# RMS norms of a two-layer S5/FoX decoder trunk: root on VectorE, first half early, S5 input matrices a tile ahead

## The chip, the core and the metric

The kernel runs on one core of a Trainium2 chip. A core has five engines with an instruction queue each: TensorE (PE; its weight loads are shown as PEld), VectorE (DVE), ScalarE (ACT), GpSimd (POOL) and SyncE (SP, which here only issues DMAs). The metric is the device time of one execution in microseconds; the median of several executions counts.

## The reference

One sequence of 512 tokens of 1024 channels passes through two layers. Layer 0 is an S5 state-space mixer, layer 1 a FoX (forgetting) attention; behind each stands a gated ConvFFN. Each of the four sub-layers is normed and modulated, and its output is gated and added to the residual:

```python
def rmsnorm(x, g):
    y = x32 * lax.rsqrt(jnp.mean(x32 * x32, axis=-1, keepdims=True) + EPS)
    return y * g
def adaln_params(c, w, b):
    mod = jax.nn.silu(c) @ w + b            # 1024 x 3072, per sub-layer
    shift, scale, gate = jnp.split(mod, 3, axis=-1)
def modulate(x, g, shift, scale):
    return rmsnorm(x, g) * (1.0 + scale) + shift
# S5: u = h @ w_in; a diagonal complex recurrence per group of 16 channels;
#     y = gelu(y + d_skip * u); y = y * sigmoid(y @ w_glu); y @ w_out
# FoX: softmax attention with a decay bias; ConvFFN: silu(conv3(a)) * b, then w_down
```

A last RMS norm without modulation (gain `final_g`) gives the output. All of it is float32.

## The kernel before

**Layout.** The residual `h` lies with channels on partitions: 8 tiles of 128 channels by 512 tokens. A norm's sum over channels is therefore a sum over partitions and tiles, made on TensorE; its result, one number a token, has to come back as a row that is equal on all partitions. Tokens are also taken in two halves of 256.

**Products.** Nearly all products are made in three passes of split operands (`w_hi·a_hi`, `w_hi·a_lo`, `w_lo·a_hi`; the matmuls of line 228). Weights come through `raw`, ScalarE makes the high part (line 211), VectorE the low part (line 212). The products of the S5 mixer's input (line 854) and the small S5 products are plain float32.

**Norms.** `add_residual` (line 290) adds a tile to `h`, `square` squares it on ScalarE and sums squares on VectorE into `ssq` (lines 282 and 284). `rms_stats` (line 299) makes the column sums on TensorE (line 307, matmuls with one output column), ScalarE takes them out of PSUM with the mean and epsilon (`v`, line 312), and GpSimd works out the inverse root from an integer first guess and two correction steps (lines 316 to 327) and writes 128x128 diagonals `dg` (line 330). Only for the second half of the last norm is VectorE used in its place. `rms_rows` (line 333) multiplies a matrix of ones with the diagonals, which gives the row (line 336). `norm_mod`'s `apply` (line 344) then does eight tiles: VectorE scales by gain and row (line 353), ScalarE adds the shift and makes the high part (line 356), VectorE the low part (line 357).

**Order at a norm.** The last product ahead of a norm works its two last weight tiles half by half (`tail`, lines 259 to 271). Between the halves stands the first half's `rms_stats`; after the second half, first `apply` of half 0 (its row matmul in it), then `rms_stats` of half 1. Half 1's `apply` is kept back (`pending`) and put in by `finish_norm` after the first 12 k-steps of the next product. A scheduler makes the final order in each engine's queue from this program order and from `issue_after`.

**The start.** `x` comes by four DMAs. The squares of the eight tiles are summed four and four on GpSimd and VectorE (line 820) and two sums go to `rms_stats` (line 307). VectorE meanwhile works through the S5 parameters (`s5_params`, lines 459 to 610), hundreds of small operations on 128x32. `ada_pe` (line 144) takes the conditioning's shift and scale, 16 weight tiles of 512 KB through three rings of buffers, on TensorE (line 155), two thirds side by side in four column groups; the 512-wide result is transposed to columns (`ada_columns`, lines 120 to 137; transposes line 126, VectorE's sum with the bias line 129). Then VectorE scales 16 tiles of 128x256 (line 840) and ScalarE adds the shift (line 843).

**The S5 loop.** For m = 0..7 (groups of 128 channels) the program order is: `s5_inputs(m)` (VectorE makes `x` from tables, lines 664 and 680; TensorE line 692; ScalarE takes `w` and `kt` out, lines 699 and 703; `kt` goes to memory `z` and comes back as Toeplitz tiles `tw`, which ScalarE masks into `t`, line 716), `outputs(m-1)` (TensorE lines 773 with `t`, 781 with the states; ScalarE's gelu, line 787, result to memory `yd`), `inputs(m+2)` (the product, line 854), some steps of conditioning (line 155: the third for the gate alone, in two column groups, then two thirds of the next sub-layer), `s5_scan(m)` (TensorE line 731) and the state output tables. `parts` reads `yd` back turned (`yt`) and splits it (lines 869 and 870), and `glu_head` works the first four glu tiles as parts arrive (line 228). The last tile's outputs, parts and glu steps come at the end with nothing behind them to fill TensorE.

**The end.** `norm_out` (line 363): ScalarE multiplies by the gain (line 373), the row is copied out (line 376), GpSimd (and for the second half VectorE too) multiplies with the row (line 380), and eight DMAs write the output channel-major (line 382).

## Time and profile before

| | |
|---|---|
| median of 3 runs | 1293.18 us (1292.35 to 1293.24) |
| profiled execution | 1296.91 us, of which the span of the trace is 1295.1 us |
| mean granted TensorE clock | 0.986 |
| VectorE, ScalarE, GpSimd instructions | 1343, 932, 215 |
| DMA | 183.11 MB, mean 141 GB/s |

The span is the time from the first to the last instruction of the profiled execution; what lies around it is 1.8 us. "Busy" is the sum of an engine's instruction times. In the rows that follow, `<-` names the instruction that ended a wait, `x` the number of instructions, and the last numbers of a windows row are the granted clock, the busy share of the DMA engines, and GB/s. A plain float32 matmul leaves two records, a split one a record for each of its three passes.

### The profile page before, as it was taken

The numbers are of one execution on the slowest core, as the hardware profiler recorded it, in microseconds if no ns is written. First come the engines' busy times: TensorE is split into PE (matmuls) and PEld (weight loads), VectorE is DVE, ScalarE is ACT, GpSimd is POOL, SyncE is SP. The second block draws the span as 40 slices with busy tenths as digits, with TensorE's granted clock in tenths as the row PEclk, the third lists the DMA queues.
The fourth block names the chain that finished last, engine by engine and source line by source line (L and its number), as shares of the span: only waits on it lengthen the run. The fifth ranks groups of instructions, "written<-read, shape, count | busy, mean of one in ns | idle before, by whom it ended". The sixth has DMA issues, their size and how long they took to land.

```text
span 1295.1 us, 17586 instructions
## 1 busy us (share of the span) xinstructions
PE 1246.3 (96%) x6728; PEld 1006.1 (78%) x6728; DVE 773.0 (60%) x1343; ACT 507.8 (39%) x932; POOL 98.6 (8%) x215
## 2 busy tenths in 40 slices
PE   4999999999999999999999999999999999999995
PEld 1466687898777778778899787878888888888885
DVE  8989975468665546765556567655754433444333
ACT  2344644334333223333333566644533312333331
POOL 3000000010000000000020243320200000000003
PEclk9999997999999999999999999999999999999998
DMA  9887665317665656655504433323233234332221
GB/s 350 294 260 212 185 189 165 109 55 212 213 187 154 187 145 220 194 160 157 157 2 132 154 123 127 97 70 98 63 119 92 68 92 133 95 96 85 73 66 65
DMA packets 74083, 183.11 MB, mean 141 GB/s; under 512 B 23079, under 2 KB 27519, under 8 KB 72975
## 3 DMA queue, kind: packets, MB, share of 16 engines
q1 hardware_dynamic: 73999, 181.99, 45.5%
q8 instruction: 53, 0.87, 0.3%
q14 instruction: 31, 0.25, 0.1%
HBM read 175.04 MB, written 6.92 MB: 140 GB/s over the span
## 4 chain that ended last, share of the span: by engine, by line
PE 70%; ACT 5%; DVE 4%; DMA 3%; issue 2%; POOL 2%; POOLq 0%; ACTq 0%; DVEq 0%; SPq 0%
PE mmp L228 64%; PE mmp L991 2%; ACT s L1102 2%; PE aux L1133 2%; DVE w_lo L212 1%; DMA raw<-in_w_up 1%; ACT w_hi L211 1%; PE aux L1116 1%; POOL hg L380 1%; PE aux L185 0%; DMA raw<-in_fox_qk 0%; ACT v L211 0%; DVE s L1098 0%; DVE ot L1140 0%; DMA raw<-in_ada_w 0%
## 5 line engine op out<-in xcount | busy, mean ns | idle before, releaser
L228 PE MATMUL mmp<-a_hi,w_hi 128*128 128x512 f32 (+1 forms) x944 | 363.6, 386 | 2.8 <-ACT a_hi L869 2.5
L228 PE MATMUL mmp<-a_lo,w_hi 128*128 128x512 f32 (+1 forms) x944 | 360.3, 382 | 0.9 <-DVE a_lo L870 0.9
L228 PE MATMUL mmp<-a_hi,w_lo 128*128 128x512 f32 (+1 forms) x944 | 360.4, 382 | 0.0
L212 DVE TENSOR_TENSOR w_lo<-raw,w_hi 128x1024 fp32r<-128x1024 f32 (+3 forms) x201 | 223.8, 1115 | 219.5 <-ACT w_hi L211 216.4
L211 ACT ACTIVATE w_hi<-raw 128x1024 fp32r<-128x1024 f32 (+3 forms) x201 | 194.6, 971 | 406.7 <-PE mmp L228 272.8
L228 PEld LDWEIGHTS mmp<-a_hi,w_hi 128*128 128x128 f32 x944 | 179.3, 190 | 43.0 <-issue 5.9
L228 PEld LDWEIGHTS mmp<-a_hi,w_lo 128*128 128x128 f32 x944 | 179.6, 190 | 34.0
L228 PEld LDWEIGHTS mmp<-a_lo,w_hi 128*128 128x128 f32 x944 | 179.6, 190 | 33.8 <-DVE a_lo L870 1.7
L228 PE MATMUL mmp<-ghi,w_hi 128*128 128x512 f32 (+1 forms) x396 | 147.5, 372 | 0.0
L228 PE MATMUL mmp<-glo,w_hi 128*128 128x512 f32 (+1 forms) x396 | 147.2, 372 | 0.0
L228 PE MATMUL mmp<-ghi,w_lo 128*128 128x512 f32 (+1 forms) x396 | 147.0, 371 | 0.0
L290 DVE SCALAR_TENSOR_TENSOR h<-mmp,par,h 128x512 f32<-128x512 f32 (+1 forms) x56 | 37.4, 673 | 110.2 <-PE mmp L228 110.1
L228 PEld LDWEIGHTS mmp<-ghi,w_hi 128*128 128x128 f32 x396 | 74.9, 189 | 15.8 <-issue 1.7
L228 PEld LDWEIGHTS mmp<-glo,w_hi 128*128 128x128 f32 x396 | 74.9, 189 | 14.1
L228 PEld LDWEIGHTS mmp<-ghi,w_lo 128*128 128x128 f32 x396 | 74.9, 189 | 14.0
L316 POOL TENSOR_SCALAR rs_i<-rs_v 128x2 int32<-128x2 int32 (+1 forms) x8 | 1.9, 235 | 1018.4 <-ACT rs_v L312 1018.4
L179 DVE SCALAR_TENSOR_TENSOR ada_acc<-raw,sc,ada_acc 128x1024 f32<-128x1024 f32 x49 | 62.7, 1280 | 19.3 <-DMA raw<-in_ada_w 19.0
L404 DVE SCALAR_TENSOR_TENSOR conv<-mmp,conv_wb,conv 128x511 f32<-128x511 f32 (+1 forms) x88 | 65.3, 745 | 4.3 <-ACT conv L402 3.1
L411 DVE TENSOR_TENSOR conv<-conv,mmp 128x512 f32<-128x512 f32 x44 | 30.0, 685 | 56.0 <-PE mmp L228 52.9
L854 PE MATMUL mmp<-a_x,raw 128*128 128x512 f32 (+1 forms) x144 | 58.2, 552 | 0.7 <-ACT a_x L843 0.7
L407 ACT ACTIVATE conv<-conv 128x512 f32<-128x512 f32 x44 | 27.6, 630 | 66.2 <-DVE conv L404 66.0
L854 PEld LDWEIGHTS mmp<-a_x,raw 128*128 128x128 f32 x144 | 26.2, 190 | 23.9 <-issue 21.2
(244 smaller groups left out, 1618.8 us busy)
## 6 DMA issues: line engine op xcount, KB each, us to landing
raw<-in_ada_w SPq DMA_DIRECT2D x96, 512.0 KB, 4.5
raw<-in_w_up SPq DMA_DIRECT2D x88, 512.0 KB, 3.6
raw<-in_w_down SPq DMA_DIRECT2D x32, 384.0 KB, 3.2
raw<-in_w_down SPq DMA_DIRECT2D x32, 320.0 KB, 3.0
nf<-nfd SPq DMA_DIRECT2D x8, 1152.0 KB, 5.7
raw<-in_fox_qk SPq DMA_DIRECT2D x16, 512.0 KB, 3.9
h<-in_x SPq DMA_DIRECT2D x8, 512.0 KB, 6.8
raw<-in_s_w_in SPq DMA_DIRECT2D x8, 512.0 KB, 7.6
```

Source lines behind the costliest of these rows:

```text
L179: nc.vector.scalar_tensor_tensor(acc, w, self.sc[:, k:k + 1], acc, op0=ALU.mult, op1=ALU.add)
L211: nc.scalar.activation(hi, src, AF.Copy)
L212: nc.vector.tensor_tensor(lo, src, hi.bitcast(F32), ALU.subtract)
L228: self.last_mm = self.nc.tensor.matmul(o, wt, xt[:, cols], start=(k == 0 and n == 0), stop=(k == nk - 1 and n == 2),)
L290: self.nc.vector.scalar_tensor_tensor(self.h[:, m, cols], ps, self.par[i][:, 16 + m:17 + m], self.h[:, m, cols], op0=ALU.mult, op1=ALU.add,)
L404: nc.vector.scalar_tensor_tensor(t[:, d:], ps[:, :S - d], cw[:, 2 - d, f:f + 1], t[:, d:], op0=ALU.mult, op1=ALU.add)
L407: nc.scalar.activation(t, t, AF.Silu)
L411: nc.vector.tensor_tensor(t, t, ps, ALU.mult)
L854: nc.tensor.matmul(ps[:, c], w[:, k, :], x[:, k, c], start=(k == 0), stop=(k == KT - 1))
L991: self.last_mm = nc.tensor.matmul(ps[q, b][:, :n], xt[:, k, tb], wt, start=(k == 0 and i == 0), stop=(k == KT - 1 and i == 2),)
L1102: nc.scalar.activation(s[:, r], s[:, r], AF.Exp, scale=-1.0, bias=mn[:, r:r + 1], accum_out=sm[:, 0, r:r + 1])
L1133: nc.tensor.matmul(pv[:, c * P:], self.v[:, hp, k, r].rearrange("p t d -> p (t d)"), pp[:, r, c + 3 * k:NB + 3 * k, :].rearrange("p b t -> ...
```

## The change

- **Root on VectorE.** `rms_stats` no longer uses ScalarE and GpSimd: `inv_root` makes `v` and the root by eleven VectorE operations straight from PSUM. `rms_rows` now broadcasts the root `y` as weights against the identity, one 128x128 matmul for each block of 128 tokens, and no diagonals are written.
- **Early first half.** In `product`'s tail the rows of half 0 are made ahead of the last weight tile of half 1, and `rms_stats` of half 1 stands ahead of half 0's `apply`.
- **First norm.** All eight tiles are squared on ScalarE and summed by 32 one-column matmuls on TensorE. The scale's third of the conditioning comes first; VectorE scales `h` into `x` as 8 tiles of 128x512; the shift's third follows, and ScalarE adds it in place.
- **Conditioning of one third** now takes rows k and k+4 at a time in four column groups; `ada_columns` adds the two partial results.
- **S5 inputs a tile ahead.** `outputs(m-1)` comes first in the loop, then `s5_inputs(m+1)`; `t` has three buffers, `dd` one, `ub` shares a buffer with `m1`. `x` is made by two 128x1024 operations in place of four of 128x512, with another layout of `bb`. The fill of `rr` moves from GpSimd to ScalarE. The conditioning's steps a tile are 2, 2, 1, 1, 1, 1, 2, 2 of the larger steps.
- **Last norm.** First half: the product with the row is on VectorE alone. Second half: TensorE transposes the gained tiles to tokens on partitions, and the root is applied as a per-partition scale when they leave PSUM, two pieces on ScalarE and two on VectorE. Each half leaves by four DMAs of 256 KB; the output's layout follows.

The diff, cut to its core:

```diff
--- before.py
+++ after.py
...
     def ada_pe(self, i, thirds):
...
+        one = len(thirds) == 1
+        steps = [[(thirds[0], k), (thirds[0], k + KT // 2)] for k in range(KT // 2)] if one else [
+            [(t, k) for t in thirds] for k in range(KT)
+        ]
...
+        for step in steps:
+            for j, (t, k) in enumerate(step):
                 w = self.raw([P, D], self.io["ada_w"][i, k * P:(k + 1) * P, t * D:(t + 1) * D], n % 3)
                 n += 1
                 for q in range(2):
                     qq = 2 * j + q
                     self.last_mm = nc.tensor.matmul(
                         ps[32 * qq:32 * qq + 32, :], self.sc32[:, k, :], w[:, q * S:(q + 1) * S],
-                        start=(k == 0), stop=(k == KT - 1), tile_position=(0, 32 * qq), skip_group_check=True,
+                        start=(step is steps[0]), stop=(step is steps[-1]), tile_position=(0, 32 * qq),
+                        skip_group_check=True,
                     )
...
             for c in HALVES:
                 for m in last:
+                    if c is HALVES[1] and m == last[-1]:
+                        rb = self.rms_rows(y)
                     ps = self.mm.tile([P, S // 2], F32, name="mmp")
                     for k in range(nk):
                         self.mms(ps, wk[m], x, k, nk, c)
                     evac(m, ps, c)
-                if c is HALVES[1]:
-                    after[1](HALVES[0], st)
-                st = after[0](c)
-            self.pending = lambda: after[1](HALVES[1], st)
+                if c is HALVES[0]:
+                    y = after[0](c)
+                else:
+                    y2 = after[0](c)
+                    after[1](HALVES[0], y, rb)
+            self.pending = lambda: after[1](HALVES[1], y2)
...
-    def rms_stats(self, cols, eng=None, dg=None):
+    def rms_stats(self, cols):
...
-        v = self.small.tile([P, nb], F32, name="rs_v")
-        nc.scalar.activation(v, ps, AF.Identity, scale=1.0 / D, bias=self.eps)
-        y, t, q = (self.small.tile([P, nb], F32, name=f"rs_{n}") for n in "ytq")
-        yi = self.small.tile([P, nb], I32, name="rs_i")
-        e = eng or nc.gpsimd
-        e.tensor_scalar(yi, v.bitcast(I32), -0.5, float(0x5F3759DF), op0=ALU.mult, op1=ALU.add)
-        y0 = yi.bitcast(F32)
-        e.tensor_tensor(t, y0, y0, ALU.mult)
+        return self.inv_root(ps, nb)
+    def inv_root(self, ps, nb):
+        v, r, t, y = (self.small.tile([P, nb], I32 if n == "r" else F32, name=f"rs_{n}") for n in "vrty")
+        e = self.nc.vector
+        e.tensor_scalar(v, ps, 1.0 / D, EPS, op0=ALU.mult, op1=ALU.add)
+        e.tensor_scalar(r, v.bitcast(I32), -0.5, float(0x5F3759DF), op0=ALU.mult, op1=ALU.add)
...
+        e.scalar_tensor_tensor(t, t, -1.25 / 0.375, t, op0=ALU.add, op1=ALU.mult)
+        e.tensor_scalar(t, t, 0.375, 1.875, op0=ALU.mult, op1=ALU.add)
+        e.tensor_tensor(y, r, t, ALU.mult)
...
-        dg = dg or self.tmp.tile([P, nb, P], F32, name="rs_dg", bufs=1)
+        return y
+    def rms_rows(self, y, nb=NB // 2):
+
+        rb = self.aux.tile([P, nb * P], F32, name="aux")
         for b in range(nb):
-            e.tensor_scalar(dg[:, b, :], self.ident, y[:, b:b + 1], 1.0, op0=ALU.mult, op1=ALU.mult)
-        return dg
-
-    def rms_rows(self, dg):
-
-        rb = self.aux.tile([P, S // 2], F32, name="aux")
-        self.nc.tensor.matmul(rb, self.ones, dg.rearrange("p b t -> p (b t)"), start=True, stop=True)
+            self.nc.tensor.matmul(
+                rb[:, b * P:(b + 1) * P], y[:, b:b + 1].to_broadcast([P, P]), self.ident,
+                start=(b == 0), stop=True, skip_group_check=True,
+            )
         return rb
...
-        def apply(cols, dg, rb=None):
...
             hi, lo = x
-            rb = rb or self.rms_rows(dg)
+            rb = rb or self.rms_rows(y)
...
     def norm_out(self, out):
...
-
-        def stats(cols):
-            return self.rms_stats(cols, nc.vector if cols is HALVES[1] else None)
-
-        def apply(cols, dg):
+
+        nc = self.nc
+
+        def apply(cols, y, rb=None):
             last = cols is HALVES[1]
             hg = self.act.tile([P, KT, S // 2], F32, name="hg", tag="a_hi" if last else "a_lo")
+            if not last:
+                for k in range(KT):
+                    nc.scalar.activation(hg[:, k], self.h[:, k, cols], AF.Copy, scale=self.final_g[:, k:k + 1])
+                for k in range(KT):
+                    nc.vector.tensor_tensor(hg[:, k], hg[:, k], rb, ALU.mult)
+                    if k % 2:
+                        nc.sync.dma_start(out[0][:, k - 1:k + 1], hg[:, k - 1:k + 1])
+                return
+            turned = [[pl.tile([P, S], F32, name=n) for pl, n in ((self.mm, "mmp"), (self.aux, "aux"))] for _ in range(2)]
             for k in range(KT):
                 nc.scalar.activation(hg[:, k], self.h[:, k, cols], AF.Copy, scale=self.final_g[:, k:k + 1])
-            rb = self.rms_rows(dg)
-            rs = self.tmp.tile([P, S // 2], F32, name="nm_h", bufs=3)
-            nc.scalar.activation(rs, rb, AF.Copy)
-            for k in range(KT):
-                on_pool = k % 3 == 0 if last else True
-                eng, r = (nc.gpsimd, rs) if on_pool else (nc.vector, rb)
-                eng.tensor_tensor(hg[:, k], hg[:, k], r, ALU.mult)
-                if k % 2:
-                    nc.sync.dma_start(
-                        out[k - 1:k + 1, :, cols].rearrange("k p t -> p k t"), hg[:, k - 1:k + 1]
+                for b in range(2):
+                    nc.tensor.transpose(
+                        turned[b][k // 4][:, k % 4 * P:(k % 4 + 1) * P], hg[:, k, b * P:(b + 1) * P], self.ident
                     )
-
-        return (stats, apply), None
+            o = self.act.tile([P, 2, 2, S], F32, name="o_tok", tag="a_lo")
+            for b in range(2):
+                nc.scalar.activation(o[:, b, 0], turned[b][0], AF.Copy, scale=y[:, b:b + 1])
+                nc.vector.tensor_scalar(o[:, b, 1], turned[b][1], y[:, b:b + 1], None, op0=ALU.mult)
+                for j in range(2):
+                    (nc.scalar if j == 0 else nc.sync).dma_start(out[1][:, b, j], o[:, b, j])
+
+        return (self.rms_stats, apply), None
...
     def s5_inputs(self, m):
...
-        x, x2 = self.s5_outer(m, self.lr, self.bb[:, 1:3], self.li, self.bb[:, 0:2], ("x", "x2"))
+
+        qs = slice(m * (GM // 2), (m + 1) * (GM // 2))
+        sh = [P, GM // 2, 2 * CG, L]
+        x, x2 = (pool.tile([P, GM // 2, 2, CG, L], F32, name=n, bufs=1 if n == "x" else 2) for n in ("x", "x2"))
+        for o, l, a in ((x, self.lr, 1), (x2, self.li, 0)):
+            nc.vector.tensor_tensor(
+                o.rearrange("p k r c j -> p k (r c) j"), l[:, qs, None, :].to_broadcast(sh),
+                self.bb[:, qs, a:a + 2, :].rearrange("p k r c -> p k (r c)")[:, :, :, None].to_broadcast(sh), ALU.mult,
+            )
         nc.vector.tensor_tensor(x, x, x2, ALU.add)
...
-        return t[:, ::-1, :].rearrange("p i b -> p b i")
+        return t[:, ::-1, :]
...
-        tok = lambda t: t.rearrange("p (b i) -> p b i", i=L)
+        tok = lambda t: t.rearrange("p (b i) -> p i b", i=L)
...
-                self.acc = self.tmp.tile([P, S], F32, name="ssq", bufs=1)
-                more = self.s5q.tile([P, 2, S], F32, name="s5_norm", tag="tw", bufs=1)
-                self.acc_last, dg = more[:, 0], more[:, 1].rearrange("p (b t) -> p b t", b=NB)
-                for k in range(KT // 2):
-                    for acc, j, eng in ((self.acc, k, nc.gpsimd), (self.acc_last, k + KT // 2, nc.vector)):
-                        sq = self.tmp.tile([P, S], F32, name="nm_t") if k else acc
-                        nc.scalar.activation(sq, self.h[:, j, :], AF.Square)
-                        if k:
-                            eng.tensor_tensor(acc, acc, sq, ALU.add)
-                self.rms_stats(slice(0, S), None, dg)
+                ps = self.aux.tile([P, NB], F32, name="aux")
+                for k in range(KT):
+                    sq = self.tmp.tile([P, S], F32, name="nm_t")
+                    nc.scalar.activation(sq, self.h[:, k, :], AF.Square)
+                    for b in range(NB):
+                        nc.tensor.matmul(
+                            ps[:, b:b + 1], sq[:, b * P:(b + 1) * P], self.ones[:, 0:1],
+                            start=(k == 0 and b == 0), stop=(k == KT - 1), skip_group_check=True,
+                        )
+                y = self.inv_root(ps, NB)
...
-                for _ in self.ada_pe(i, (0, 1)):
+                for _ in self.ada_pe(i, (1,)):
                     last = self.last_mm.ins
+                with tc.issue_after(last):
+                    rb = self.rms_rows(y, NB)
+                x = self.act.tile([P, KT, S], F32, name="a_x", tag="a_hi")
+                for k in range(KT):
+                    applied = nc.vector.scalar_tensor_tensor(
+                        x[:, k], self.h[:, k], self.ga[i][:, k:k + 1], rb, op0=ALU.mult, op1=ALU.mult
+                    ).ins
+                for _ in self.ada_pe(i, (0,)):
+                    pass
+                for k in range(KT):
+                    nc.scalar.activation(x[:, k], x[:, k], AF.Identity, bias=self.par[i][:, k:k + 1])
                 wi = {m: self.raw([P, KT, P], self.io["s5_w_in"][m], m % 3) for m in range(2)}
                 self.s5_turns(keep, co, si)
-                with tc.issue_after(last):
-                    rows = [self.rms_rows(dg[:, q:q + 2]) for q in (0, 2)]
-                x = self.act.tile([P, KT, S], F32, name="a_x", tag="a_hi")
-                for c, rb in zip(HALVES, rows):
-                    for k in range(KT):
-                        t = self.tmp.tile([P, S // 2], F32, name="nm_h", bufs=3)
-                        applied = nc.vector.scalar_tensor_tensor(
-                            t, self.h[:, k, c], self.ga[i][:, k:k + 1], rb, op0=ALU.mult, op1=ALU.mult
-                        ).ins
-                        nc.scalar.activation(x[:, k, c], t, AF.Identity, bias=self.par[i][:, k:k + 1])
...
-                for c in (HALVES if m == 0 else (slice(0, S),)):
-                    for k in range(KT):
-                        nc.tensor.matmul(ps[:, c], w[:, k, :], x[:, k, c], start=(k == 0), stop=(k == KT - 1))
+                for k in range(KT):
+                    nc.tensor.matmul(ps, w[:, k, :], x[:, k], start=(k == 0), stop=(k == KT - 1))
...
             ada = [self.ada_pe(i, (2,)), self.ada_pe(i + 1, (0, 1))]
             for m in range(2):
                 inputs(m)
+            with tc.issue_after(applied):
+                ws[0] = self.s5_inputs(0)
             for m in range(KT):
+                if m:
+                    outputs(m - 1)
                 with tc.issue_after(applied):
-                    ws[m] = self.s5_inputs(m)
                     if m % 2 == 0:
                         self.s5_tables(slice(m * 4, m * 4 + 8), 3, 6)
-                if m:
-                    outputs(m - 1)
+                    if m + 1 < KT:
+                        ws[m + 1] = self.s5_inputs(m + 1)
                 if m + 2 < KT:
                     inputs(m + 2)
-                for _ in range(4 if m < 2 else 2):
+                for _ in range((2, 2, 1, 1, 1, 1, 2, 2)[m]):
                     next(ada[m >= 2], None)
                 sts[m] = self.s5_scan(m, ws[m][0], us[m])
                 with tc.issue_after(applied):
```

More of the change, by code (lines that the diff above doesn't have):

```diff
@@ L123, in ada_columns @@
         n = (c1 - c0) // 4
+        r = rows.shape[0]
         ps = self.aux.tile([P, NB, P], F32, name="aux")
         for b in range(NB):
-            nc.tensor.transpose(
-                ps[:, b, :32 * n], rows[:32 * n, b * P:(b + 1) * P], self.ident[:32 * n, :32 * n]
-            )
-        nc.vector.tensor_tensor(
-            self.par[i][:, c0:c1].rearrange("p (q b) -> p q b", b=NB),
-            ps.rearrange("p b (q r) -> p q b r", r=32)[:, :n, :, 0],
-            self.ada_b[:, i, c0:c1].rearrange("p (q b) -> p q b", b=NB), ALU.add,
-        )
+            nc.tensor.transpose(ps[:, b, :r], rows[:, b * P:(b + 1) * P], self.ident[:r, :r])
+        par = self.par[i][:, c0:c1].rearrange("p (q b) -> p q b", b=NB)
+        add = self.ada_b[:, i, c0:c1].rearrange("p (q b) -> p q b", b=NB)
+        for h in range(r // (32 * n)):
+            nc.vector.tensor_tensor(
+                par, ps.rearrange("p b (q r) -> p q b r", r=32)[:, h * n:(h + 1) * n, :, 0], add, ALU.add
+            )
+            add = par
         if c0 <= 8 and c1 >= 16:
@@ L713, in s5_inputs @@
         )
-        t = pool.tile([P, GM, CG, L], F32, name="t", bufs=2)
+        t = pool.tile([P, GM, CG, L], F32, name="t", bufs=3)
         for i in range(L):
```

53 lines of the change are left out of this document (25 added, 28 removed).

## The prediction

> **What bounds the kernel now.** I read the page first: busy times, then the chain that ended last.
>
> ```profile
> PE 1246.3 (96%) x6728; PEld 1006.1 (78%) x6728; DVE 773.0 (60%) x1343; ACT 507.8 (39%) x932; POOL 98.6 (8%) x215
> ...
> PE 70%; ACT 5%; DVE 4%; DMA 3%; issue 2%; POOL 2%; POOLq 0%; ACTq 0%; DVEq 0%; SPq 0%
> ```
>
> TensorE is busy 1246.3 of 1295.1 us, and this change takes little from its matmuls. Only time in which TensorE waits or runs at half clock is to be won: before its first product, at the end of the S5 mixer, at each norm, and after the last product. So the second view is the list of TensorE's waits:
>
> ```profile
> PE aux L307 <- DVE e L478: 17.3, 1, 17.3
> PE aux L336 <- DVE rs_dg L330: 6.1, 1, 6.1
> PE mmp L228 <- ACT a_hi L869: 2.5, 1, 2.5
> PE aux L336 <- POOL rs_dg L330: 2.4, 4, 1.0
> ```
>
> One wait of 17.3 us at the start, 6.1 us in the last norm, 2.4 us in all at the other norms. The profiled execution took 1296.91 us (span 1295.1), 3.73 above the median of 1293.18. I sum against the profiled one and subtract 3.73 at the end. A measurement of this kernel can tell about 0.2%, 2.6 us, from no change.
>
> **Part 1: the start.** TensorE's rows by time, then ScalarE's first square and VectorE's rows (start, duration, count):
>
> ```profile
> 17.28 1.87 PE L307 MATMUL aux<-ones,ssq 128*128 128x1 f32 x8 [17.28 <-DVE e L478]
> 19.23 1.87 PE L307 MATMUL aux<-ones,s_norm 128*128 128x1 f32 x8
> 21.03 7.58 PE L155 MATMUL mmp<-raw,sc 128*32 128x512 f32 x40
> ...
> 39.31 14.04 PE L854 MATMUL mmp<-a_x,raw 128*128 128x256 f32 x48 [0.73 <-ACT a_x L843]
> ...
> 5.44 0.63 ACT L818 ACTIVATE ssq<-h 128x512 f32<-128x512 f32 x1 [2.52 <-DMA h<-in_x]
> ...
> 12.78 0.18 DVE L485 SCALAR_TENSOR_TENSOR e<-e,e 128x32 f32<-128x32 f32 x1
> ...
> 35.63 0.62 DVE L610 TENSOR_TENSOR s_li<-s_w,s_w 128x256 f32<-128x256 f32 x1
> ...
> 38.24 6.36 DVE L840 SCALAR_TENSOR_TENSOR nm_h<-h,ga,aux 128x256 f32<-128x256 f32 x16
> 44.51 1.29 DVE L664 TENSOR_TENSOR x<-s_lr,s_bb 128x512 f32<-128x512 f32 x2
> ...
> 47.12 1.22 DVE L680 TENSOR_TENSOR x<-x,x 128x1024 f32<-128x1024 f32 x1
> ```
>
> Before, VectorE works without a gap through one chain of small operations on the S5 parameters until 36.25 (35.63 + .62), and the shift and scale columns reach it just after, so the product L854 starts at 39.31.
>
> After, the squares are summed by 32 matmuls of one column (L841), eight groups of four, and VectorE's v (L325 of the changed kernel) stands about a third of the way down that chain, with all of its later instructions queued behind it. VectorE would reach it near 12.6 (the chain's L485 of 12.78, less the sum L820 that goes). When is L841 done? A group of four (eight records) took 1.87 us twice running, or 1.80 by the last start. If that holds, eight groups take 14.4 us, and from 6.1, when the first square is there (5.44 + .63), they end at 20.5. If they run at half of it, VectorE hardly waits. So VectorE resumes between 12.6 and 20.7. I take 20.7: the 1.87 us row is this very form at this very place, and the second group was no quicker than the first. From L325 to the end of the chain were 36.25 − 12.78 = 23.5 us; less two sums of .7, a stretch of POOL's making and the row and table work that moves, plus eleven small operations of inv_root, I count 18.9. So the chain ends at 39.6 (at 31.5 if L841 is quick) where it ended at 36.25.
>
> Behind it VectorE has, ahead of the shift column: two columns (.7), eight scalings L860 of 128x512 (at .65 to .68 by L664's 1.29 for two: 5.3, for L840's 6.36), two 128x1024 for x (2.4 by L680's 1.22) and their sum (1.2), tables, and the shift's add: in the order of its instructions 13.4 in all. ScalarE then adds the shift, .6 a tile, and the product (L878) starts .7 later: 53.7 (45.6 if quick), 14.4 later than 39.31. This is the price of the change at this place. VectorE is what TensorE waits for there, so that the third of the scale comes 1 us later through its ring of three buffers costs nothing; were VectorE free, the DMA would be next.
>
> *A rule against this step's price.* The Trainium skill, "TensorE: Matmul & The Clock Gate", section "What's actually happening", has the clock rise after one free-running window of about 3.4 us in which TensorE was kept busy. By it L841 would warm within 3.4 to 6.8 us and end near 16, not 20.5. The trace speaks rather against: the two L307 groups fill 3.6 us and the weights product behind them needs 7.58 us for its first 40 records. It is the first rival below.
>
> **Part 2: the S5 mixer.** What TensorE saves until the mixer's end:
>
> ```profile
> 62.29 3.63 PE L155 MATMUL mmp<-raw,sc 128*32 128x512 f32 x16
> 99.56 1.92 PE L155 MATMUL mmp<-raw,sc 128*32 128x512 f32 x16
> 53.28 2.02 PE L692 MATMUL aux<-s_rr,x 64*128 64x80 f32 x32
> ```
>
> The gate's third takes 32 records in two column groups, 2 × 3.63; in four, 2 × 1.92: −3.4. The first L692 group, 2.0, now runs before the product, in TensorE's idle time. The rest of the product work is the same. What it waits for at the end:
>
> ```profile
> 158.76 1.31 PE L692 MATMUL aux<-s_rr,x 64*128 64x80 f32 x10 [1.38 <-ACT kt L703]
> 160.00 3.67 PE L773 MATMUL aux<-u,t 128*128 128x64 f32 x16
> 188.67 2.57 ACT L716 ACTIVATE t<-tw,first 128x128 f32<-128x128 f32 x8 [8.36 <-DMA tw<-s_z]
> 191.29 2.00 PE L773 MATMUL aux<-u,t 128*128 128x64 f32 x16 [1.53 <-ACT t L716]
> 193.22 3.29 PE L781 MATMUL aux<-ua,w 64*128 64x63 f32 x32
> 204.07 0.79 PE L228 MATMUL mmp<-a_hi,w_hi 128*128 128x512 f32 x1 [2.51 <-ACT a_hi L869]
> 160.00:192.00 32.00, 30.47 (x262) 26.38 (x262) 23.89 (x37) 15.72 (x45) 0.00 (x0) 0.90 0.62 187
> 192.00:210.00 18.00, 15.21 (x69) 12.08 (x69) 4.28 (x4) 5.79 (x9) 0.00 (x0) 0.64 0.38 108
> ```
>
> Waits: 1.38 + 1.53 + 2.51 = 5.4. Half clock: .10 of 32 us and .36 of 18 us, 9.7 in all (L773's 3.67 for 2.00 shows it). Together 15.1. All of it is the last tiles' chain kt, z, tw, t (a trip through memory) that is not ready, and later yt's trip. With the input matrices made a tile earlier, about 16 us, that chain has its time, and the last L805 has 63 glu matmuls behind it to hide yt. But this holds only if VectorE keeps a tile ahead, and it is full too:
>
> ```profile
> 96.00:128.00 32.00, 32.00 (x286) 20.43 (x286) 28.96 (x49) 13.44 (x46) 0.00 (x0) 1.00 0.69 205
> 128.00:160.00 32.00, 30.05 (x248) 18.38 (x247) 29.18 (x47) 18.71 (x47) 0.00 (x0) 0.99 0.61 178
> ```
>
> 29 of 32 us: it starts 3.4 later than before and gains at most 3 us in each 32. TensorE starts 14.4 later, so VectorE has at first a tile in hand. The mixer's end was near 209.7. After: 209.7 + 14.4 − 2.0 − 3.4, plus 2.5 as TensorE idles before the product and starts it at half clock (5 us of it), is 221.2 if all stalls stay, 206.1 if all go. I choose nearly all, as the chain's slack is a whole tile: 13 of 15.1, so 208.2: **−1.5**. Both ends: −3.6 and +11.5; with a quick L841 8.1 less, −11.7.
>
> **Part 3: the three norms between.** POOL's chain is replaced by VectorE's; the half-0 rows come ahead of the last tail tile. Rows of the three places:
>
> ```profile
> 277.95 1.26 DVE L353 SCALAR_TENSOR_TENSOR nm_h<-h,ga,aux 128x256 f32<-128x256 f32 x3
> ...
> 284.19 0.74 DVE L177 TENSOR_SCALAR ada_acc<-raw,sc 128x1024 f32<-128x1024 f32 x1
> ...
> 289.19 1.27 DVE L179 SCALAR_TENSOR_TENSOR ada_acc<-raw,sc,ada_acc 128x1024 f32<-128x1024 f32 x1
> 910.00:914.00 4.00, 3.67 (x18) 3.59 (x18) 4.00 (x11) 2.71 (x7) 1.92 (x8) 0.57 0.12 43
> ```
>
> Half 0's apply (before from 277.95, a row matmul behind the last tail tile) has its row a tail tile earlier; it still shares VectorE with the last residual and v, so I let its product start 1.6 to 2 us sooner, an estimate. Against it, half 1's eleven root operations (about .2 each as the chain's .18, some 2 us) now stand on VectorE among 16 apply operations of .42 (1.26 for three) and the conditioning operations of .74 and 1.27. After the mixer this makes half 1's first a_lo some 2 us later than the product needs it: **+1.7** net. Before FoX there is no conditioning work: **−0.8** (its share of the four waits, 2.4 us, and a little more). Before the last ConvFFN TensorE ran at .57 of its clock from 910 to 914, 1.7 us, and took the longest of those waits, up to 1.0; some of this stays: **−2.2**. Sum −1.3; ends −5 (all three as the last) and +5 (all three as the first).
>
> **Part 4: the end.**
>
> ```profile
> 1279.45 0.50 PE L307 MATMUL aux<-ones,ssq 128*128 128x1 f32 x4
> ...
> 1280.12 5.50 POOL L380 TENSOR_TENSOR hg<-hg,nm_h 128x256 f32<-128x256 f32 x8 [3.61 <-ACT nm_h L376]
> 1281.39 0.17 DVE L316 TENSOR_SCALAR rs_i<-rs_v 128x2 int32<-128x2 int32 x1 [1.69 <-ACT rs_v L312]
> ...
> 1281.67 0.55 DVE L318 TENSOR_TENSOR rs_t<-rs_i 128x2 f32<-128x2 f32 x1
> ...
> 1286.26 0.16 DVE L327 TENSOR_TENSOR rs_y<-rs_y,rs_t 128x2 f32<-128x2 f32 x1
> ...
> 1287.06 1.22 PE L336 MATMUL aux<-rs_dg,ones 128*128 128x256 f32 x2 [6.06 <-DVE rs_dg L330]
> ...
> 1288.78 2.09 POOL L380 TENSOR_TENSOR hg<-hg,nm_h 128x256 f32<-128x256 f32 x3 [3.17 <-ACT nm_h L376]
> ```
>
> While POOL scales the first half (1280.12 to 1285.62) VectorE's operations of two columns take .55 to .66 us, afterwards .16. POOL's work goes; eleven operations spaced .21 are 2.3 us from about 1281.1 (v's chain began at 1281.39), y at 1283.7 with a scaling between, for 1286.42. Then four scalings out of PSUM, two on each engine, about .65 each, so the last leaves at 1285.4. Before, y led to the diagonals, the row matmul, the copy and the products until 1290.9 (1288.78 + 2.09), 5.5 later than 1285.4. The sixteen transposes run while y is computed. The four last DMAs carry 256 KB each like the four before, .5 us more in flight: **−5.0** [−3.5, −6.5].
>
> **Sum.** −1.5 − 1.3 − 5.0 = −7.8: 1289.1 for a profiled execution, 1285.4 for the median.
>
> **Rivals.**
> *Quick column sums* (the clock rises in L841, the rule above, or VectorE is early): part 1 gives up to 8.1 back, taken 6.4 for an end near 15: 1279.0. For it: four records took .50 us at 1279.45, half of the start's pace, right behind the last product. Against: 1.87 for eight twice at the start. Chance .24.
> *VectorE late all through* (the other side): L841 ends at 20.5, and VectorE, 29 of 32 us busy, never wins the tile it should be ahead, so that the chain of the last tile comes no earlier relative to TensorE and the stalls stay: +11.5 − 1.3 − 5.0 = +5.2, 1298.4. It is slower as soon as fewer than some 5 of the 15.1 us of stalls go. Chance .20.
> *The norms cost what the first norm does*: half 1's chain behind half 0's apply in all three places, +5 for −1.3: 1291.7. For it: 16 × .42 of apply in the same queue. Chance .12.
> *My forecast*: .44.
>
> **Chances and range.** Faster by over .2%: .44 + .24 = .68. Within: .12. Slower: .20. The range reaches from the quick case with norms and end at their good ends (1279.0 − 3.7 − 1.5 = 1273.8) to the slower rival: 1274 to 1299.
>
> **What would show it.** The end of the 32 L841 matmuls and the start of L325 (20.5 / 12.6); L878's start (53.7 / 45.6); no idle time before the last L797 and clock 1.0 from 160 to 210; the glu head's end near 208; half 1's first matmul in each norm; y at 1283.7 on the old scale, and small VectorE operations at .2 in the end. I am wrong if stalls at the end of S5 move to other tiles, or if ScalarE, which gets the shift and the copies of bb, becomes late.

## The result and the profile after

The changed kernel takes 1302.69 us (median of 7 runs, 1297.44 to 1306.40) against 1293.24 for the kernel before (7 runs, 1290.79 to 1297.01). The ratio is 1.0071, 95% interval 1.0049 to 1.0092: it is slower by 9.5 us. The forecast was 1285.4, the range 1274 to 1299; the time lies outside it, on the other side. The profiled executions span 1302.9 and 1295.1 us, 7.8 apart, so the traces hold most of the difference.

Four landmarks cut both traces into pieces: the last matmul of the glu head (its end, which the prediction took for the end of the S5 mixer); the matmul of the attention's output product that waits 2.06 us for the last piece of attention (its tile lies in the buffer of `v`); the last matmul of the last product; the end of the span. First before, then after (start, duration, engine, line):

```profile
209.58 0.63 PE L228 MATMUL mmp<-a_hi,w_lo 128*128 128x512 f32 x1
...
881.34 0.50 PE L228 MATMUL mmp<-v,w_hi 128*128 128x512 f32 x1 [2.06 <-ACT v L211]
...
1278.90 0.28 PE L228 MATMUL mmp<-ghi,w_lo 128*128 128x256 f32 x1
```

```profile
224.48 0.39 PE L233 MATMUL mmp<-a_hi,w_lo 128*128 128x512 f32 x1
...
898.31 0.50 PE L233 MATMUL mmp<-v,w_hi 128*128 128x512 f32 x1 [2.06 <-ACT v L216]
...
1292.61 0.28 PE L233 MATMUL mmp<-ghi,w_lo 128*128 128x256 f32 x1
```

| piece | before | after | difference |
|---|---|---|---|
| start to the glu head's end (start and S5 loop) | 210.2 | 224.9 | +14.7 |
| to the output product's matmul (two norms in it) | 671.1 | 673.4 | +2.3 |
| to the last matmul (third norm in it) | 397.6 | 394.3 | −3.3 |
| to the end (last norm) | 16.2 | 10.3 | −5.9 |

All norms between and at the end together gain 6.9 us. The whole loss, and more, lies ahead of the first of them. TensorE's longest waits after:

```profile
PE aux L126 <- ACT ada_rows L167: 9.3, 3, 6.9
PE aux L716 <- DVE x L704: 6.5, 1, 6.5
PE aux L841 <- DVE e L492: 6.1, 1, 6.1
PE mmp L233 <- ACT w_hi L216: 4.0, 1, 4.0
```

The 17.3 us wait at the start is now 6.1, but the three others, of which before had only .8 us (for `ada_rows`), make 19.8 us. All but 5.6 us of that lies ahead of the input product, and the start's rows show where it comes from, TensorE's first and then VectorE's and ScalarE's:

```profile
6.05 13.81 PE L841 MATMUL aux<-ones,nm_t 128*128 128x1 f32 x64 [6.05 <-DVE e L492]
19.80 5.23 PE L160 MATMUL mmp<-raw,sc 128*32 128x512 f32 x32
31.97 1.12 PE L126 MATMUL aux<-rest,ada_rows 128*128 128x128 f32 x4 [6.95 <-ACT ada_rows L167]
...
40.07 0.66 PE L126 MATMUL aux<-rest,ada_rows 128*128 128x128 f32 x4 [0.75 <-ACT ada_rows L167]
...
52.07 16.52 PE L878 MATMUL mmp<-a_x,raw 128*128 128x512 f32 x32
```

```profile
11.77 0.18 DVE L492 TENSOR_SCALAR e<-e 128x32 f32<-128x32 f32 x1
19.90 0.16 DVE L325 TENSOR_SCALAR rs_v<-aux 128x4 f32<-128x4 f32 x1 [7.96 <-PE aux L841]
...
36.92 0.64 DVE L626 TENSOR_TENSOR s_li<-s_w,s_w 128x256 f32<-128x256 f32 x1
...
38.09 5.36 DVE L860 SCALAR_TENSOR_TENSOR a_x<-h,ga,aux 128x512 f32<-128x512 f32 x8
43.37 1.22 DVE L700 TENSOR_TENSOR x<-s_lr,s_bb 128x1024 f32<-128x1024 f32 x1
...
49.85 0.15 DVE L130 TENSOR_TENSOR par<-aux,rest 128x8 f32<-128x8 f32 x1
```

VectorE stands still for 7.96 us behind the column sums with about a third of its parameter chain done (first two rows). Later the transposes that bring the shift's columns are through at 40.7 (40.07 + .66), but VectorE adds the bias only at 49.85, behind the scalings and the first input matrices. So the input product begins at 52.07 in place of 39.31. ScalarE is drawn in: a copy for the scan waits there for a VectorE result until 30.16, and the conditioning's rows, ready earlier, stand behind it:

```profile
30.16 1.28 ACT L772 ACTIVATE cf<-s_mask,s_mag 128x128 f32<-128x128 f32 x4 [10.34 <-DVE s_mag L475]
31.35 0.57 ACT L167 ACTIVATE ada_rows<-mmp 128x512 f32<-128x512 f32 x1
```

12.8 us of the 14.7 are there at 52.07, before the input product has begun. The rest, and the savings that did not show, are in the loop.

### The profile page after: what moved, and what is told of

The parts are those of the page before. It is cut to its first block, busy times and chain, and to the rows that moved or that the text cites. A ratio compares the mean times of both kernels' runs of the same rounds, so it can differ in the third digit from the quotient of the medians.

```text
span 1302.9 us, 17657 instructions
## 1 busy us (share of the span) xinstructions
PE 1259.4 (97%) x6796; PEld 1018.4 (78%) x6796; DVE 775.1 (59%) x1410; ACT 510.1 (39%) x918; POOL 56.7 (4%) x94
## 4 chain that ended last, share of the span: by engine, by line
PE 88%; DVE 6%; ACT 3%; DMA 2%; issue 1%; SPq 0%; DVEq 0%; ACTq 0%
PE mmp L233 70%; PE mmp L878 3%; PE mmp L1018 3%; PE aux L1160 2%; DMA tw<-s_z 1%; PE aux L716 1%; PE aux L805 1%; PE aux L1143 1%; PE aux L841 1%; DVE w_lo L217 1%; PE aux L797 1%; PE aux L1113 1%; ACT w_hi L216 1%; PE aux L755 1%; ACT s L1129 1%
## 5 line engine op out<-in xcount | busy, mean ns | idle before, releaser
L233 PEld LDWEIGHTS mmp<-glo,w_hi 128*128 128x128 f32 x396 | 74.6, 188 | 14.7
L878 PE MATMUL mmp<-a_x,raw 128*128 128x512 f32 x128 | 64.2, 642 | 0.0
L233 PE MATMUL mmp<-v,w_hi 128*128 128x512 f32 (+1 forms) x160 | 42.1, 352 | 2.1 <-ACT v L216 2.1
```

Source lines behind the costliest of these rows:

```text
L233: self.last_mm = self.nc.tensor.matmul(o, wt, xt[:, cols], start=(k == 0 and n == 0), stop=(k == nk - 1 and n == 2),)
L878: nc.tensor.matmul(ps, w[:, k, :], x[:, k], start=(k == 0), stop=(k == KT - 1))
```

## The experiments

The theories. **Start**: the loss lies ahead of the input product, in VectorE's order. **Loop**: the loss comes from the new order in the S5 loop. Medians below are of the runs named, the ratio is to the kernel before on the same chip (its medians there 1293.6 to 1294.3).

**1. norms_only**: the kernel before, with `rms_stats`, `inv_root`, `rms_rows`, the tail of `product` and `norm_out` of after; the first norm keeps the old functions under other names.

> The kernel before, with only the norms between the products and the last norm as after (root on VectorE, first half's row early, output turned on TensorE); its S5 mixer, start and loop, is as before. Theory 'start' (the loss of the change lies ahead of the S5 input product: VectorE's queue stands behind the column sums and the shift's column stands behind the scalings): the norms and the end gain what the traces show between the glu head and the end, 14.7 - 7.8 = 6.9 us, so about 1286.5 for 1293.2 before. Rival 'loop' (the loss comes from the S5 loop's new order): the same number, since neither start nor loop is touched. If it is not faster than before by 4 us or more, both are wrong on the norms.

Measured: 1283.94 us (8 runs), ratio 0.9925 (0.9898 to 0.9951). The norms gain at least what was expected. Its S5 mixer has the same instructions in the same order on TensorE, ScalarE and VectorE as before, but in the profiled executions its glu head ended at 202.95, against 210.21. Before, the two traces part at 158.76, where TensorE waited 1.38 us for `kt` (here .18), and half clock followed. The window from 160 to 192 us, before (shown with the prediction) at clock 0.90 and 30.47 us busy, is here:

```profile
160.00:192.00 32.00, 31.85 (x304) 27.43 (x304) 24.16 (x37) 15.84 (x43) 0.00 (x0) 1.00 0.66 213
```

So some 7 us of the stalls that I counted as S5's were that execution's, not the program's. It was a long one of its kernel, 3.7 us above the median; this one lies 1.7 below its own.

**2. start_only**: after, with the S5 loop in the old order.

```diff
...
-            with tc.issue_after(applied):
-                ws[0] = self.s5_inputs(0)
             for m in range(KT):
+                with tc.issue_after(applied):
+                    ws[m] = self.s5_inputs(m)
+                    if m % 2 == 0:
+                        self.s5_tables(slice(m * 4, m * 4 + 8), 3, 6)
                 if m:
                     outputs(m - 1)
-                with tc.issue_after(applied):
-                    if m % 2 == 0:
-                        self.s5_tables(slice(m * 4, m * 4 + 8), 3, 6)
-                    if m + 1 < KT:
-                        ws[m + 1] = self.s5_inputs(m + 1)
...
-                for _ in range((2, 2, 1, 1, 1, 1, 2, 2)[m]):
+                for _ in range(2):
```

> The kernel after, with the S5 loop in the old order (input matrices of tile m in the tile itself, two conditioning steps a tile); start, norms and end stay as after. Theory 'start': the product still begins near 52 us on the trace, so the time stays near 1302, at 1299 to 1304. Rival 'loop': the order was the loss and the late start is made up for later, so 1287 to 1290.

Measured: 1293.17 us (12 runs), ratio 0.9997 (0.9979 to 1.0015). Between the two numbers: 9.5 us below after, 9.2 above norms_only. Neither theory alone holds.

**3. loop_only**: after, with the start of before (squares on GpSimd and VectorE, `ada_pe(i, (0, 1))`, scaling and first product in halves, first root on GpSimd).

> The kernel after, with the start of before (squares summed on GpSimd and VectorE, both thirds of the conditioning first, scaling in halves, root of the first norm on GpSimd); loop, norms and end as after. Theory 'start': the input product begins near 39.5 us again, 12.6 earlier than after, so about 1302.7 - 12.6 = 1290, or less where the loop then runs warm. Rival 'loop': 1299 or more.

Measured: 1284.47 us (6 runs), ratio 0.9925 (0.9898 to 0.9952). The old start brings back 18.2 us with the new loop, more than the 12.8 of the trace.

**4. shift_first**: after, with the tables and input matrices behind the shift's columns.

```diff
-            nc.vector.tensor_tensor(
+            self.last_col = nc.vector.tensor_tensor(
                 par, ps.rearrange("p b (q r) -> p q b r", r=32)[:, h * n:(h + 1) * n, :, 0], add, ALU.add
-            )
+            ).ins
...
                 for _ in self.ada_pe(i, (0,)):
                     pass
+                applied = self.last_col
```

> The kernel after, with one order constraint: the tables and input matrices come on VectorE behind the addition of the shift's column, which stands right behind the eight scalings. Theory 'start': the column was ready near 40.7 us but added at 49.9; now it is added near 43.5, the product begins near 45 in place of 52, so about 1302.7 - 7 = 1296, 1295 to 1298. Rival 'loop': no gain over 1 us, the input matrices being 0.5 us later.

Measured: 1293.21 us (12 runs), ratio 0.9991 (0.9973 to 1.0008): 9.5 us below after from the place of two additions of .15 us. The product begins at 44.36.

**5. root_late_shift_first**: the same, and the first root behind the parameters.

```diff
-                y = self.inv_root(ps, NB)
                 co, si, params = self.s5_params(keep, tp, self.first["s5_prm"])
+                with tc.issue_after(params):
+                    y = self.inv_root(ps, NB)
```

> The kernel shift_first, and besides the first norm's root comes on VectorE behind the S5 parameters in place of in the middle of them. Theory 'queue' (VectorE stands behind the column sums from 12.6 to 20 us with its parameters undone): the parameters end some 7 us sooner, near 31, the input product begins near 39 in place of 44.4, so about 1293.2 - 5 = 1288. Rival 'other engines' (the conditioning's matmuls or their DMAs set the start): the product still begins near 44 and the time stays at 1293.

Measured: 1288.72 us (11 runs), ratio 0.9957 (0.9941 to 0.9973). Another 4.5 us, as expected, though the product begins only at 41.25.

```profile
41.25 14.00 PE L880 MATMUL mmp<-a_x,raw 128*128 128x512 f32 x32 [1.22 <-ACT a_x L868]
```

Together the two orders on VectorE bring back 14.0 us of the 18.2 between after and loop_only. The product also takes 14.00 us for 16.52: the granted clock over its time is 1.00, and .85 in after.

**6. loop_pairs**: loop_only, with the next tile's input matrices ahead of the last tile's outputs.

```diff
-                if m:
-                    outputs(m - 1)
                 with tc.issue_after(applied):
...
                     if m + 1 < KT:
                         ws[m + 1] = self.s5_inputs(m + 1)
+                if m:
+                    outputs(m - 1)
```

Its reason is in TensorE's rows of loop_only, where the small matmuls come in pieces between the product's:

```profile
104.68 1.11 PE L758 MATMUL aux<-s_rr,x 64*128 64x80 f32 x8
105.73 1.12 PE L920 MATMUL mmp<-a_x,raw 128*128 128x512 f32 x2
106.78 2.82 PE L758 MATMUL aux<-s_rr,x 64*128 64x80 f32 x24
```

In norms_only 32 of these records take 2.02 to 2.95, here 8 take 1.05 to the next start. They use half of TensorE's rows each, and in the program's order the upper and the lower half take turns. The queue's order shows that in the new loop pieces of four matmuls stand together that use the same half. I suppose that the outputs hold PSUM buffers which the other half needs; no run shows it.

> The kernel loop_only with two blocks of the S5 loop exchanged: the input matrices of the next tile stand ahead of the outputs of the last one, still a tile ahead. In loop_only 88 of the 128 input-matrix matmuls follow one of the same half of TensorE's rows in the queue, 38 here, 36 before. Theory 'pairs' (two matmuls on different rows run beside each other only when they are neighbours, 0.125 us a matmul against 0.26): their time in the S5 mixer falls from 25.4 to about 20.5 us, and the kernel from 1284.5 to about 1279.5. Rival 'ahead' (being a tile ahead itself costs, by PSUM buffers or by VectorE): the time stays at 1283 to 1286.

Measured: 1282.43 us (6 runs), ratio 0.9907 (0.9884 to 0.9930). The time of that line falls as expected (busy time of the line alone, loop_only and loop_pairs):

```profile
38.00:204.00 166.00, 26.13 (x256) 23.20 (x256) 0.97 0.68 211
```

```profile
38.00:204.00 166.00, 20.78 (x256) 19.20 (x256) 0.94 0.68 212
```

5.35 us less in the line, but only 2.0 in the median, within the intervals. The two rows show where the rest went in these executions: clock .97 and .94 over 166 us is some 5 us more at half clock, and near the loop's end a wait of 4.1 us for the glu weights' low part stands where loop_only waits 2.6. In the queue, 66 of the 128 matmuls of loop_only and 26 of loop_pairs follow one of the same half (the expectation's 88 and 38 count every matmul of such a piece, its first one too). So a lost pair costs 5.35 / 40 = .13 us in the line; that the kernel gains as much is not shown. The Trainium skill, "TensorE: Matmul & The Clock Gate", section "The mechanism", says that weight loads overlap running matmuls only if they go to another group of rows. The trace agrees: 8 records of one group took 1.05 us, .13 each, where 32 strictly in turn took 2.02, .06 each.

**7. late_start_old_loop**: root_late_shift_first with the loop of start_only.

> The kernel root_late_shift_first with the S5 loop in the old order. If start and loop are the two losses of the change and add up: the product begins near 39 as in norms_only, and the conditioning's third in four column groups saves 3.4 us of TensorE, so about 1283.9 - 3.4 = 1280.5. If the start still costs: 1285 or more. If the new loop were no loss: the same as root_late_shift_first.

Measured: 1281.01 us (6 runs), ratio 0.9899 (0.9879 to 0.9918), as expected where start and loop are the two losses. The product begins at 40.36.

**8. warm_start**: after, with 14 matmuls ahead of the column sums whose result is not used.

```diff
+                warm = self.mm.tile([P, S], F32, name="mmp")
+                for _ in range(14):
+                    nc.tensor.matmul(warm[:, :P], self.ones, self.ones, start=True, stop=True)
                 ps = self.aux.tile([P, NB], F32, name="aux")
```

> The kernel after, with 14 matmuls of 128x128 ones on TensorE ahead of the column sums (some 6 us at half clock, in time in which it has nothing to do; their result is not used). Theory 'one-column matmuls run at half clock because nothing woke TensorE, and do not keep it awake': the sums begin near 7 us, run quick for one to two windows of about 3.4 us and then slow again, so they end between 12 and 18 in place of 19.9 and the kernel gains 2 to 6 us: 1297 to 1301. Rival 'one-column matmuls take 0.43 us whatever the clock': the sums end at 20 to 21, the time stays at 1302 or is 1 us more.

Measured: 1297.46 us (12 runs), ratio 1.0020 (1.0003 to 1.0037): 5.2 us below after. Its rows and its clock (last but two) in three windows inside the sums:

```profile
6.61 11.22 PE L844 MATMUL aux<-ones,nm_t 128*128 128x1 f32 x64
```

```profile
7.00:10.40 3.40, 3.40 (x28) 3.40 (x28) 2.90 (x16) 1.90 (x3) 0.00 (x0) 0.85 1.06 405
10.40:14.00 3.60, 3.60 (x18) 3.60 (x19) 1.27 (x8) 1.26 (x2) 0.00 (x0) 0.50 1.03 410
14.00:17.00 3.00, 3.00 (x15) 3.00 (x16) 0.00 (x0) 2.46 (x5) 0.00 (x0) 0.50 1.03 407
```

TensorE is busy all through, without a gap, and its clock falls to half within the sums: 28 records in 3.4 us, then 18 in 3.6. A gapless row of one-column matmuls did not hold the clock up. The product begins at 50.04, 2.0 us earlier than in after; where the rest of the 5.2 us comes from I did not settle.

**9. ada_early**: after, with the conditioning's steps at two a tile (`range(2)`).

> The kernel after with the conditioning's steps in the S5 loop back at two a tile, so that they end with the sixth tile in place of the eighth. In every kernel with the new loop TensorE waits some 4 us near the loop's end for the split of the first glu weights, whose loads start at 177 to 187 us in after and at 143 to 169 in start_only. Theory 'late glu weights' (the conditioning's last tiles stand ahead of them in SyncE's queue and in the buffers): the wait of 3.97 us goes, and the half clock behind it, so about 1302.7 - 6 = 1297. Rival 'splits' (ScalarE and VectorE are late with the split, wherever the loads stand): 1301 to 1304.

Measured: 1299.48 us (12 runs), ratio 1.0037 (1.0020 to 1.0055). The first glu weight's load starts at 149.49 in place of 177.51, and the wait of 3.97 us is gone from the list. The gain is 3.2 us in the median, half of what I expected and hardly clear of the intervals: TensorE now waits 2.0 us for the last tile's `yt` instead.

**10. after_pairs_ada**: after with the edits of 6 and 9.

> The kernel after with ada_early's steps and with the next tile's input matrices ahead of the last tile's outputs (38 of 128 matmuls follow one of the same rows, 72 in after). If lost pairs and late glu weights are what the new loop costs, the time comes down to start_only's 1293 or below it, 1290 to 1294. If being a tile ahead is itself the cost: 1297 or more.

Measured: 1294.37 us (12 runs, 1291.85 to 1302.55), ratio 1.0006 (0.9985 to 1.0026): 8.3 of the 9.5 us between after and start_only, some 4 us either way by the intervals. Most of the loop's loss behind the late start, if not all, comes from these two places in the order.

**11. all_mended**: the edits of 4, 5, 6 and 9.

> The change with its four losses mended: root behind the S5 parameters, shift's column right behind the scalings, input matrices ahead of the outputs, conditioning's steps two a tile. The tile-ahead loop then against late_start_old_loop's 1281.0: if being a tile ahead gains what the change was predicted to gain at the end of S5 (the last tile's chain), 1272 to 1277; if not, 1280 to 1284.

Measured: 1281.30 us (5 runs), ratio 0.9894 (0.9878 to 0.9911). It equals late_start_old_loop's 1281.01, which has the old loop. Being a tile ahead, with its side effects mended, gains nothing that can be measured. What TensorE waits for at the end of S5 is still there:

```profile
PE mmp L233 <- ACT a_hi L895: 4.3, 1, 4.3
```

**12. norms_third**: norms_only, with the third for the gate in four column groups, the new form of the input matrices and the constants' fill on ScalarE; first norm, conditioning at the start and loop order as before.

> Start and S5 loop in the old order as in norms_only, norms and end as after, and of the changes in the S5 mixer only those of form: a third of the conditioning in four column groups, the input matrices by two operations of 128x1024. If the reworked start (column sums on TensorE, scaling ahead of the shift) is worth anything once mended, this is slower than all_mended and late_start_old_loop (1281.0 to 1281.3): 1283 or more. If the start is worth nothing, norms_only's 1283.9 less the 3.4 us of the four groups: 1279.5 to 1281.5.

Measured: 1281.23 us (4 runs), ratio 0.9905 (0.9887 to 0.9923). The start of before is as good as the mended new one.

## Why the prediction was wrong

**The start (part 1) was right.** Column sums to 20.5 forecast, 19.86 measured (6.05 + 13.81); VectorE held from 12.6, measured 11.95; the parameters' end 39.6, measured 37.56; the product at 53.7, measured 52.07, and 2.5 us lost to half clock there, as 16.52 against 14.00 shows. What I did not see is that ScalarE would stand behind a VectorE result too (10.34 us); it did not set the end. Nor did I see that the late start would cost more than its landmark: 18.2 us with the new loop. I put the chance of quick column sums at .24; warm_start shows that even a woken TensorE does not stay quick through them.

**The S5 mixer (part 2) was wrong, and with it the sign.** The step that failed is "I choose nearly all, as the chain's slack is a whole tile: 13 of 15.1". Forecast −1.5, measured +14.7. The waits that I named did go: those of before for `kt`, `t` and `yt` (1.4, 1.5 and 2.5 us) are not in after's list. But TensorE lost as much in other places. In the loop it waited 1.6 us for conditioning rows and 4.0 for glu weights, 5.6 for the 5.4 of before, and at clock .93 over the 173 us from the product on (the first of the four rows under "The loop's price") some 12 us went to half clock, 2.5 of them at the product itself, for the 9.7 that I had counted. Three things stand behind this.

- The stalls were not all the program's. With the same instruction order norms_only's glu head ended 7.3 us sooner. I took one execution's half clock for a fixed cost. I even took it off twice: once as stalls that go, and once, in all likelihood, in the 3.73 us that the profiled execution lay above the median.
- What remains is not the chain kt, z, tw, t. In norms_only, late_start_old_loop and all_mended the one long wait at the end is for the last tile's `yt` (a_hi, 4.4, 4.0 and 4.3 us), which comes after the last outputs and which earlier input matrices do not shorten. I had written that 63 glu matmuls would cover it. In after it does not show, because the glu weights came late and the glu head was then still at work.
- The new order costs TensorE itself: the input matrices' matmuls took 27.55 us in after, 20.74 before (busy time of the line). Of these 6.8 us the new order makes 3.8, as start_only, with the old order behind the same start, took 23.74. I said that the rest of the product work was the same, counting matmuls and not their neighbours in the queue.

```profile
45.00:225.00 180.00, 27.55 (x256) 24.48 (x256) 0.91 0.62 193
```

```profile
38.00:210.00 172.00, 20.74 (x256) 19.11 (x256) 0.94 0.67 208
```

**The slower rival** had the right sign, the late start with no stall won back (mixer's end at 221.2; the glu head ended at 224.87). That its sum comes within 4 us is luck: some 7 us of the stalls that it keeps were one execution's, and new losses took their place. Its mechanism, a VectorE that never wins its tile, isn't what the runs showed: mending the pairs and the place of the weights' loads, with VectorE's work the same, brought 8.3 us. Its bound of +11.5 for the mixer was no bound, as nothing in it allowed for new stalls.

**The norms and the end (parts 3 and 4) came out near.** First two norms +2.3 (forecast +.9), third −3.3 (−2.2), last −5.9 (−5.0). After the mixer the forecast wait is there, 1.5 us for `a_hi` and .4 for `a_lo`, and some 1.7 us of half clock behind it (clock .79 and .78 from 304 to 308 and to 312) that I had not counted there. The root of the last norm after:

```profile
1294.65 0.16 DVE L325 TENSOR_SCALAR rs_v<-aux 128x2 f32<-128x2 f32 x1 [1.23 <-PE aux L316]
...
1296.62 0.16 DVE L336 TENSOR_TENSOR rs_y<-rs_y,rs_t 128x2 f32<-128x2 f32 x1
```

With GpSimd out of the way, all eleven operations take .16 or .17, 2.1 us in all; y is there 4.2 us behind the start of the last matmul (1296.78 − 1292.61), 7.5 before (1286.42 − 1278.90). That norms_only gains 10 us at the median, and the pieces of the trace 6.9, is within its interval of 6.3 to 13.2.

**The loop's price and what stays open.** With the gate's third in four groups in all of them, the four combinations are 1281.2 (old start, old loop), 1284.5 (old, new), 1293.2 (new, old) and 1302.7 (new, new). The new loop costs 3.3 us behind the early start and 9.5 behind the late one. Lost pairs do not explain this difference: 66 matmuls in the first and 54 in the second follow one of the same half. Half clock does, in the profiled executions. These rows go from the product's start to the glu head's end in after, start_only, loop_only and norms_third:

```profile
52.00:225.00 173.00, 166.98 (x1196) 108.02 (x1194) 121.08 (x184) 73.85 (x203) 0.00 (x0) 0.93 0.62 192
52.00:215.00 163.00, 157.11 (x1200) 102.62 (x1199) 124.01 (x186) 75.42 (x207) 0.00 (x0) 0.97 0.65 205
38.00:205.00 167.00, 164.06 (x1240) 111.20 (x1240) 133.61 (x212) 76.38 (x213) 0.00 (x0) 0.97 0.67 210
38.00:202.00 164.00, 158.98 (x1241) 107.86 (x1241) 135.53 (x213) 77.07 (x217) 0.00 (x0) 0.97 0.69 215
```

Reckoned as in the prediction, 12.1 us went to half clock in the first and 4.9 to 5.0 in the others, so 7.2 of the 10 us by which the new loop is longer behind the late start, and none of the 3 behind the early one. The median clock over all runs agrees: .982 for after and .988 for start_only, .9945 for both loop_only and norms_third. In after_pairs_ada the clock is .98 again over the 161 us from 52 on, so the two places in the order bring the half clock with them. Why they do so behind a late start and not behind an early one stays open.

## What to carry to other kernels

An operation that waits for another engine holds everything behind it in its queue: before placing one in the middle of a chain, ask when its input comes, and place short operations that release the busiest engine ahead of long ones that don't. A stall seen in one execution's trace is only worth what it costs in several. Whoever moves work a step ahead should look at what it is then next to: here matmuls on the two halves of TensorE's rows lost their neighbours, and weights lost their place in the load queue. That cost up to 9.5 us, and the move itself gained nothing that could be measured.

## What the hardware showed that I had not expected

- A gapless row of one-column float32 matmuls let a woken TensorE fall back to half clock (0.85, then 0.50, in warm_start). That the sums of after ran at half clock throughout is read from their pace, 13.81 us for 64 records or .22 each, against .12 and then .20 in warm_start; the trace of after has no clock change ahead of 23 us.
- Two matmuls of 64 rows ran beside each other when they were neighbours in the queue: 32 records in 2.02 us strictly in turn, 8 in 1.05 of one half.
- The same instruction order of the S5 mixer ended 7.3 us apart in two executions, at clock 0.90 and 1.00 in the same 32 us.
